# A feed-forward stage with seven block products in place of eight, and its down projection as a second pass

## The chip, the cores and the metric

The kernel runs on one core of a Trainium2 chip. The metric is the device time of one execution in microseconds (us). One run in the profiler comes with a trace of every instruction on the core's engines: TensorE (PE, matmuls; its weight loads PEld), VectorE (DVE), ScalarE (ACT), GpSimd (POOL) and SyncE (SP, which here only issues DMAs).

## The reference, cut to what matters

The whole is a two-block transformer on 1024 rows (S) of 1024 columns (D) in float32. The change concerns the feed-forward part of the first block, with F = 2816 hidden columns:

```
h = h + xo.reshape(b, s, XA_HEADS * XA_HEAD_DIM) @ xa_w_o[l]

fn = rms_norm(h, norm_ffn[l])
g = fn @ ffn_w_gate[l]
g_pad = jnp.pad(g, ((0, 0), (CONV_W - 1, 0), (0, 0)))
cw = ffn_conv_w[l]
g_conv = ffn_conv_b[l] + sum(cw[i] * g_pad[:, i:i + s] for i in range(CONV_W))
h = h + (jax.nn.silu(g_conv) * (fn @ ffn_w_up[l])) @ ffn_w_down[l]
```

The convolution has three taps along the rows. Cross-attention stands ahead of this part, the second block's even layer behind it.

## The kernel before, in words

Every float32 matmul is made of three passes (`mm3`, lines 258 to 265): each operand is split into a high half, cast by ScalarE, and a low half, the difference, made by VectorE or GpSimd. The passes are high x high, high x low, low x high, all with 128 rows of weights and 512 moving columns, summed in a PSUM bank. `load_w` does this for weights: a DMA on SP (line 192), the cast on ACT (line 197), the subtraction (line 202) with 66% of the columns on DVE and the rest on POOL.

`norm_T` (line 224) scales the rows of h by their norm, transposes them on PE (line 250) and splits them (`split`, ACT line 211, DVE line 212) into X: 8 k blocks of 128 x 1024, high and low. `ffn` (line 312) then goes through F in 11 groups of 256 columns. For each group it loads gate and up weights (two loads of 512 KB each) and two blocks of down weights. For each of the two f tiles of 128 hidden columns PE makes gate into a two-bank PSUM tile `pb` (48 matmuls), ACT adds the bias and the third tap (line 329), DVE the other two taps from PSUM (line 331), ACT the silu (line 333); PE makes up (48 matmuls), DVE multiplies (line 336), ACT and POOL split y into halves (lines 339, 340). The down projection of the group before stands between the gate products: `out_proj` makes 16 banks of 6 matmuls, and DVE adds each to h in place (line 290), which stays in SBUF throughout. The list of instructions is put into an order for each engine by a scheduler that goes by program order and priorities (`later` shifts a part of it); a DMA queue and an engine take what they have in that order, and an instruction that waits holds up all behind it.

Behind the stage, the next one stores h in `hs` (line 1815), norms and transposes it, and reads its own weights `a_w_in` and small convolution weights by SP.

## Time and profile before

| | |
|---|---|
| median of 3 runs | 3114.76 us (3112.94 to 3118.19) |
| the profiled run | 3115.11 us |
| its span in the trace | 3113.4 us, mean granted TensorE clock 0.984 |
| busy: TensorE, VectorE, ScalarE, GpSimd | 2959.9, 1958.0, 1128.7, 839.4 us |
| DMA | 228.44 MB, 73 GB/s over the span |
| feed-forward stage, from its first transpose to the next stage's | 758.62 to 1499.00 us |

The profile's page sums the run; the views of the trace behind it show a stretch of time (windows), single instructions on an engine in order of time with the idle time before each and what ended it (timeline), and groups of instructions by line and shape (lines). A matmul's printed duration is the time from its start to its modelled end; matmuls overlap, so their spacing is read from counts in a window or from starts.

### The profile page before, as it was taken

Reading aid. Unit: us, or ns where it says so; the run is one execution under the profiler, and the core shown is the slowest. Engines: PE = TensorE matmul, PEld = TensorE weight load, DVE = VectorE, ACT = ScalarE, POOL = GpSimd, SP = SyncE. Lnnn points to the kernel's source line nnn. Section 1 sums busy time; section 2 is a strip of 40 time slices with the busy share of each in tenths; the row PEclk is TensorE's granted clock in tenths of the full one; section 3 lists DMA queues with packets and bytes.
Section 4 is the critical chain, followed back from the end, with each engine's and each line's share of the span. In section 5 each row is a group of like instructions: output and inputs, shape, how many; then the busy total and the mean of one; then the engine's idle time right before and its main releaser. Section 6 shows DMA issues by size and latency. Waiting matters only on the chain.

```text
span 3113.4 us, 38565 instructions
## 1 busy us (share of the span) xinstructions
PE 2959.9 (95%) x14726; PEld 2413.3 (78%) x14734; DVE 1958.0 (63%) x3129; ACT 1128.7 (36%) x2090; POOL 839.4 (27%) x754
## 2 busy tenths in 40 slices
...
DMA packets 167565, 228.44 MB, mean 73 GB/s; under 512 B 15293, under 2 KB 105941, under 8 KB 167381
## 3 DMA queue, kind: packets, MB, share of 16 engines
...
q8 instruction: 116, 1.90, 0.3%
...
## 4 chain that ended last, share of the span: by engine, by line
PE 68%; DVE 14%; issue 5%; POOL 4%; DMA 3%; ACT 3%; SPq 0%; POOLq 0%; DVEq 0%; ACTq 0%
PE pa_t L263 11%; PE pa_t L264 11%; PE pa_t L265 11%; PE pb_t L265 8%; PE pb_t L264 8%; PE pb_t L263 8%; DVE acc_t L1144 3%; PE pa_t L774 2%; PE pb_t L869 1%; DVE wl_t L202 1%; PE pa_t L888 1%; PE pb_t L1583 1%; DVE h_t L290 1%; DMA wr_t<-in_c_w_in 1%; PE pb_t L1584 1%
## 5 line engine op out<-in xcount | busy, mean ns | idle before, releaser
L202 POOL TENSOR_TENSOR wl_t<-wr_t,wh_t 128x349 fp32r<-128x349 f32 (+2 forms) x221 | 296.9, 1346 | 1311.5 <-ACT wh_t L197 1252.6
L263 PE MATMUL pb_t<-x_t,wh_t 128*128 128x512 f32 x1312 | 518.8, 396 | 3.7 <-DVE bc_t L1184 1.1
L265 PE MATMUL pb_t<-x_t,wl_t 128*128 128x512 f32 x1312 | 516.2, 394 | 0.8 <-DVE wl_t L202 0.8
L264 PE MATMUL pb_t<-x_t,wh_t 128*128 128x512 f32 x1280 | 505.4, 395 | 0.0
L197 ACT CAST wh_t<-wr_t 128x1024 fp32r<-128x1024 f32 (+2 forms) x221 | 217.5, 993 | 546.8 <-PE pb_t L264 240.1
L202 DVE TENSOR_TENSOR wl_t<-wr_t,wh_t 128x675 fp32r<-128x675 f32 (+1 forms) x195 | 208.6, 1074 | 303.2 <-ACT wh_t L197 302.8
L263 PE MATMUL pa_t<-wh_t,x_t 128*128 128x512 f32 (+3 forms) x1024 | 374.5, 366 | 2.6 <-DVE xl_t L212 0.8
L264 PE MATMUL pa_t<-wl_t,x_t 128*128 128x512 f32 (+3 forms) x1024 | 371.3, 363 | 0.5 <-DVE wl_t L202 0.5
L1144 DVE SCALAR_TENSOR_TENSOR acc_t<-u_t,c,acc_t 128x1024 f32<-128x1024 f32 x240 | 339.7, 1417 | 2.9
L290 DVE TENSOR_TENSOR h_t<-h_t,pa_t 128x512 f32<-128x512 f32 x336 | 226.4, 684 | 147.7 <-PE pa_t L265 145.9
L263 PEld LDWEIGHTS pb_t<-x_t,wh_t 128*128 128x128 f32 x1312 | 247.6, 189 | 58.8 <-ACT x_t L211 1.9
L265 PEld LDWEIGHTS pb_t<-x_t,wl_t 128*128 128x128 f32 x1312 | 247.5, 189 | 55.6 <-DVE wl_t L202 2.1
L264 PEld LDWEIGHTS pb_t<-x_t,wh_t 128*128 128x128 f32 x1280 | 241.4, 189 | 52.7 <-DVE x_t L212 0.9
L265 PE MATMUL pa_t<-wh_t,x_t 128*128 128x512 f32 (+3 forms) x640 | 221.5, 346 | 0.0
L263 PEld LDWEIGHTS pa_t<-wh_t,x_t 128*128 128x128 f32 x1024 | 192.3, 188 | 33.9 <-ACT wh_t L197 2.2
L264 PEld LDWEIGHTS pa_t<-wl_t,x_t 128*128 128x128 f32 x1024 | 192.5, 188 | 31.3 <-DVE wl_t L202 2.2
L265 PE MATMUL pa_t<-wh_t,xl_t 128*128 128x512 f32 x512 | 200.9, 393 | 3.0 <-POOL xl_t L1681 2.1
L263 PE MATMUL pa_t<-wh_t,g_t 128*128 128x512 f32 x384 | 150.1, 391 | 2.6 <-DVE h_t L292 1.3
L264 PE MATMUL pa_t<-wl_t,g_t 128*128 128x512 f32 x384 | 149.4, 389 | 0.0
L265 PE MATMUL pa_t<-wh_t,g_t 128*128 128x512 f32 x352 | 136.8, 389 | 1.1 <-POOL g_t L340 1.1
L209 DVE TENSOR_TENSOR pt_t<-pa_t,pt_t 128x512 fp32r<-128x512 f32 (+2 forms) x240 | 119.7, 506 | 24.0 <-ACT pt_t L208 22.1
L208 ACT CAST pt_t<-pa_t 128x512 fp32r<-128x512 f32 (+2 forms) x240 | 104.8, 443 | 81.0 <-PE pa_t L774 44.9
...
## 6 DMA issues: line engine op xcount, KB each, us to landing
wr_t<-in_a_w_in SPq DMA_DIRECT2D x46, 512.0 KB
wr_t<-in_c_w_in SPq DMA_DIRECT2D x26, 512.0 KB
wr_t<-in_ffn_w_gate SPq DMA_DIRECT2D x22, 512.0 KB
wr_t<-in_ffn_w_up SPq DMA_DIRECT2D x22, 512.0 KB
wr_t<-in_ffn_w_down SPq DMA_DIRECT2D x22, 512.0 KB
h_t<-in_x SPq DMA_DIRECT2D x16, 512.0 KB
wr_t<-in_a_w_out SPq DMA_DIRECT2D x16, 512.0 KB
...
```

The costliest lines, as they stand in the source:

```text
L197: nc.scalar.copy(hi, raw)
L202: e.tensor_tensor(*[x[:, c] for x in f], op=ALU.subtract)
L208: nc.scalar.copy(hi, src)
L209: nc.vector.tensor_tensor(lo, src, hi.bitcast(F32), op=ALU.subtract)
L263: mm(out, lh, rh, start=st, stop=False)
L264: mm(out, lh, rl, start=False, stop=False)
L265: mm(out, ll, rh, start=False, stop=en)
L290: self.nc.vector.tensor_tensor(h[t][:, c], h[t][:, c], ps, op=ALU.add)
L774: self.nc.tensor.transpose(pt[:, i * 256 + q * P:i * 256 + (q + 1) * P], w[t0 + q][:, (b0 + i) * P:(b0 + i + 1) * P], self.ident)
L869: mm(sp[:, c0:c0 + wd], qT[:96, hd, t * P:(t + 1) * P], kT[:96, hd, c0:c0 + wd], start=True, stop=c0 + wd < n)
L888: mm(po[:, q:256], vhl[hd][:, kb], x[:, i * 256 + q:i * 256 + 256], start=kb == 0 and j == 0, stop=kb == t0 + 1 and j == 1)
L1144: nc.vector.scalar_tensor_tensor(acc, u[:, k:k + S], cw31(k, c), acc, op0=ALU.mult, op1=ALU.add)
```

## The change

Gate and up of a group are computed as one 256 x 1024 (weight columns x rows) result each, split 2 x 2: two halves of 128 columns, two halves of 512 rows, and the inner dimension in two halves of 512. In place of eight block products there are seven, by Strassen's scheme in Winograd's form, with weights A and activations B: A11 B11, A12 B21, S2 T2, S3 T3, S1 T1, A22 T4, S4 B22. The weight sums are S1 = A21 + A22, S2 = S1 - A11, S3 = A11 - A21, S4 = A12 - S2; the activation sums T1 = B12 - B11, T2 = B22 - T1, T3 = B22 - B12, T4 = T2 - B21. The results are sums of products, taken out of PSUM by VectorE.

`ffn_w` makes the seven weight operands of a unit (gate or up of a group) with their halves. `ffn_x` makes the activation operands; the scaled rows are made in place, so h is first stored to DRAM (`hf`). `ffn_up` runs the 22 units; y of each pair of f tiles is stored to DRAM (`yf`). `ffn_down` is a second pass: y is read back, split, and multiplied by the down weights in groups of four f tiles (12 matmuls in a bank; the last group has two tiles and 6), with h read back from `hf`. PSUM banks are single ones from `pa`. Lines behind the stage move by 167 or 176.

```diff
@@ -309,40 +309,207 @@
-    def ffn(self, h, st):
...
+    def ffn_w(self, dram, c0):
+        nc = self.nc
+        r = []
+        for i in range(2):
+            r.append(self.slot("wr", [P, 4, 256]))
+            nc.sync.dma_start(out=r[i], in_=dram[i * 512:i * 512 + 512, c0:c0 + 256].rearrange("(k p) n -> p k n", p=P))
+        a11, a21, a12, a22 = (x[:, :, o:o + P] for x in r for o in (0, P))
+        out = {}
+        v, g = nc.vector, nc.gpsimd
+        def halves(name, src, eng):
+            hi, lo = out[name] = self.slot("wh", [P, 4, P], F32R), self.slot("wl", [P, 4, P], F32R)
+            nc.scalar.copy(hi, src)
+            eng.tensor_tensor(lo, src, hi.bitcast(F32), op=ALU.subtract)
+        halves("A11", a11, v)
+        halves("A22", a22, g)
+        s1, s2, s3, s4 = a22, a11, a21, a12
+        g.tensor_tensor(s1, a21, a22, op=ALU.add)
+        g.tensor_tensor(s3, a11, a21, op=ALU.subtract)
+        g.tensor_tensor(s2, s1, a11, op=ALU.subtract)
+        halves("S2", s2, v)
+        halves("A12", a12, v)
+        g.tensor_tensor(s4, a12, s2, op=ALU.subtract)
+        halves("S3", s3, v)
+        halves("S1", s1, v)
+        halves("S4", s4, g)
+        return out
+    def ffn_x(self, h, st, hf, between):
+        nc = self.nc
+        X = {n: [[x[:, i] for i in range(2)] for x in (self.slot(tag, [P, 2, 512], F32R) for _ in range(4))]
+             for n, tag in (("B11", "x"), ("B21", "x"), ("B22", "xz"))}
+        th = {n: [self.slot("xh", [P, 512], F32R) for _ in range(4)] for n in ("T2", "T3", "T1", "T4")}
+        X.update({n: [] for n in th})
+        rows = [[self.slot("xt", [P, 512]) for _ in range(2)] for _ in range(4)]
+        gs = list(st)
+        for t in [g0 + j for g0 in gs for j in range(4)]:
+            nc.gpsimd.dma_start(out=hf[t * P:(t + 1) * P, :], in_=h[t])
+        v = nc.vector
+        def turn(g0, k):
+            ps = self.psum()
+            for j in range(4):
+                nc.tensor.transpose(ps[:, j * P:(j + 1) * P], h[g0 + j][:, k * P:(k + 1) * P], self.ident)
+            return ps
+        def halves(n, k, src, eng):
+            hi, lo = th[n][k], self.slot("xt", [P, 512], F32R)
+            X[n].append((hi, lo))
+            nc.scalar.copy(hi, src)
+            eng.tensor_tensor(lo, src, hi.bitcast(F32), op=ALU.subtract)
+        for i, g0 in enumerate(gs):
+            with self.later(0 if i else -AHEAD):
+                for j in range(4):
+                    t = h[g0 + j]
+                    if j == 3:
+                        nc.scalar.activation(t, t, AF.Copy, scale=st[g0][:, j:j + 1])
+                    else:
+                        v.tensor_scalar(t, t, st[g0][:, j:j + 1], None, op0=ALU.mult)
+                for k in range(4):
+                    c1, c2 = self.col("norm_ffn", k), self.col("norm_ffn", k + 4)
+                    p1, p2 = turn(g0, k), turn(g0, k + 4)
+                    if i == 0:
+                        for n, p, c, r in (("B11", p1, c1, rows[k][0]), ("B21", p2, c2, rows[k][1])):
+                            self.split(*X[n][k], p, c)
+                            nc.scalar.activation(r, p, AF.Copy, scale=c)
+                        continue
+                    ta, tb = (self.slot("wr", [P, 2, 512]) for _ in range(2))
+                    t1, t2, t3, t4 = ta[:, 0], ta[:, 1], tb[:, 0], tb[:, 1]
+                    b11, b21 = rows[k]
+                    v.scalar_tensor_tensor(t1, p1, c1, b11, op0=ALU.mult, op1=ALU.subtract)
+                    v.scalar_tensor_tensor(t2, p2, c2, t1, op0=ALU.mult, op1=ALU.subtract)
+                    self.split(*X["B22"][k], p2, c2)
+                    nc.gpsimd.tensor_tensor(t3, t2, b11, op=ALU.subtract)
+                    nc.gpsimd.tensor_tensor(t4, t2, b21, op=ALU.subtract)
+                    halves("T2", k, t2, v)
+                    halves("T3", k, t3, v)
+                    halves("T1", k, t1, v)
+                    halves("T4", k, t4, nc.gpsimd)
+            if i == 0:
+                between(X)
+        return X
+    def ffn_up(self, h, st, hf, yf, cw, more):
+        v = nc.vector
+        ha, hb = (slice(g0 * P, g0 * P + 512) for g0 in st)
+        units = [(x, g) for g in range(DFF // 256) for x in ("ffn_w_gate", "ffn_w_up")]
+        ws, p1 = {}, {}
+        def load(i):
+            if i < len(units):
+                ws[i] = self.ffn_w(a[units[i][0]][0], units[i][1] * 256)
+            elif i == len(units):
+                self.wd = self.down_w(0)
+        def prod(w, x):
+            ps = self.psum()
+            for k in range(4):
+                self.mm3(ps, [(w[0][:, k], w[1][:, k])], [x[k]], k == 0, k == 3)
+            return ps
+        def first(i, X):
+            p1[i] = self.slot("p1", [P, 512])
+            nc.scalar.copy(p1[i], prod(ws[i]["A11"], X["B11"]))
+        load(0)
+        load(1)
+        def between(X):
+            for i in range(2):
+                first(i, X)
+            for i in range(2):
+                p2[i] = prod(ws[i]["A12"], X["B21"])
+        p2 = {}
+        X = self.ffn_x(h, st, hf, between)
+        more()
+        gt = {}
+        for i, (kind, g) in enumerate(units):
+            gate = kind == "ffn_w_gate"
+            if gate:
+                G = [self.slot("g", [P, S]) for _ in range(2)]
+            else:
+                O = gt.pop(g)
+            def part(j, hs, u, ps, op=ALU.add):
+                x = G[j][:, hs] if gate else self.tmp(512)
+                v.tensor_tensor(x, u, ps, op=op)
+                if not gate:
+                    nc.gpsimd.tensor_tensor(O[j][:, hs], O[j][:, hs], x, op=ALU.mult)
+            def total(u, ps):
+                x = self.tmp(512)
+                v.tensor_tensor(x, u, ps, op=ALU.add)
+                return x
+            if i > 1:
+                first(i, X)
+            w = ws.pop(i)
+            u2 = total(p1[i], prod(w["S2"], X["T2"]))
+            part(0, ha, p1[i], p2[i] if i < 2 else prod(w["A12"], X["B21"]))
+            if i:
+                load(i + 1)
+            u3 = total(u2, prod(w["S3"], X["T3"]))
+            p5 = prod(w["S1"], X["T1"])
+            part(1, hb, u3, p5)
+            u4 = total(u2, p5)
+            part(1, ha, u3, prod(w["A22"], X["T4"]), ALU.subtract)
+            part(0, hb, u4, prod(w["S4"], X["B22"]))
+            if gate:
+                gt[g] = []
+                for j in (0, 1):
+                    f = 2 * g + j
+                    o = self.slot("o", [P, S])
+                    nc.scalar.activation(o, G[j], AF.Identity, scale=cw(2, f), bias=self.col("ffn_conv_b", f))
+                    for tap, sh in ((1, 1), (0, 2)):
+                        v.scalar_tensor_tensor(o[:, sh:], G[j][:, :S - sh], cw(tap, f), o[:, sh:], op0=ALU.mult, op1=ALU.add)
+                    nc.scalar.activation(o, o, AF.Silu)
+                    gt[g].append(o)
+            else:
+                for j in (1, 0):
+                    nc.sync.dma_start(out=yf[2 * g + j], in_=O[j])
+    def down_w(self, f0):
+        out = {}
+        for hf in range(2):
+            for f in range(f0, min(f0 + 4, DFF // P)):
+                out[f, hf] = self.load_w(self.a["ffn_w_down"][0], f * P, 1, hf * 512, 512), 0
+        return out
+    def ffn_down(self, hs, yf):
+        nc = self.nc
+        h, st = [], {}
+        for f0 in range(0, DFF // P, 4):
+            fs = range(f0, min(f0 + 4, DFF // P))
+            w = self.wd if f0 == 0 else self.down_w(f0)
+            for f in fs:
+                y = self.slot("yr", [P, S])
+                nc.sync.dma_start(out=y, in_=yf[f])
+                hl = [self.slot("yb" if f0 % 8 else "ya", [P, S], F32R) for _ in range(2)]
+                nc.scalar.copy(hl[0], y)
+                (nc.gpsimd if f % 2 else nc.vector).tensor_tensor(hl[1], y, hl[0].bitcast(F32), op=ALU.subtract)
+                ys.append(hl)
+            if f0 == 0:
+                h = self.load_h(hs, nc.scalar)
+            last = f0 + 4 >= DFF // P
+            for x, ts in ([(range(2), [t]) for t in range(NT)] if last else [([hf], range(NT)) for hf in range(2)]):
+                for hf in x:
+                    self.out_proj(h, ys, [w[f, hf] for f in fs], ts=ts, hfs=[hf], stats=st if last and hf else None)
+        return h, st
...
@@ -1802,8 +1969,17 @@
         if h_in is None or "B" in stages:
             mctx.close()
         if "C" in stages:
-            with K.pool("xf", x=16), K.pool("w1", wr=2, wh=6, wl=6), K.pool("ffn", g=10, tmp=2):
-                st = K.ffn(h, st)
+            hf, yf = dt("hf", [S, D]), dt("yf", [DFF // P, P, S])
+            with K.pool("wf", wr=3, wh=10, wl=10, p1=2):
+                cw = K.convw("ffn_conv_w", 3, DFF, tag="wr")
+                with K.pool("xf", x=8, xh=16, xt=16, xz=4), ExitStack() as fs:
+                    def more():
+                        hctx.close()
+                        fs.enter_context(K.open(K.pool("fg", o=2, tmp=4, g=2)))
+                    K.ffn_up(h, st, hf, yf, cw, more)
+                hctx = K.open(K.pool("h1b", "right", h=8))
+                with K.pool("fd", yr=2, ya=8, yb=8):
+                    h, st = K.ffn_down(hf, yf)
         if "D" in stages:
             with K.pool("w1", **W), K.pool("xd", usum=1, rsg=4, g=3, acc=2):
                 usum, rs = K.slot("usum", [P, S]), []
```

The removed `ffn` is printed above with the kernel before. Line numbers in what follows are those of each kernel.

The order of the instructions, first on PE where the stage begins. Line 250 is the transposes before, line 359 after; 263 to 265 are the three passes. Before:

```order
L250 MATMUL pa_t<-c_72,g_t 128x128
L263 MATMUL pa_t<-wh_t,x_t 128x512
L250 MATMUL pa_t<-c_72,g_t 128x128
L264 MATMUL pa_t<-wl_t,x_t 128x512
L250 MATMUL pa_t<-c_72,g_t 128x128
L265 MATMUL pa_t<-wh_t,x_t 128x512
L250 MATMUL pa_t<-c_72,g_t 128x128 x45
L263 MATMUL pb_t<-x_t,wh_t 128x512 x2
```

After, where the first half's transposes and then those of the second half stand:

```order
L263 MATMUL pa_t<-x_t,wh_t 128x512
L264 MATMUL pa_t<-x_t,wh_t 128x512
L265 MATMUL pa_t<-x_t,wl_t 128x512
L359 MATMUL pa_t<-c_72,h_t 128x128 x32
L263 MATMUL pa_t<-xh_t,wh_t 128x512
L264 MATMUL pa_t<-xt_t,wh_t 128x512
L265 MATMUL pa_t<-xh_t,wl_t 128x512
```

The second half's transposes have moved behind the early products of units 0 and 1 (a further 32 of line 359 stand ahead of those), where before all but a few stood together.

DVE in the middle of the stage. Before, line 331 is the taps from PSUM `pb_t`, 336 the multiplication, 290 the sum into h, 202 the low halves of weights:

```order
L202 TENSOR_TENSOR wl_t<-wr_t,wh_t 128x675 x2
L331 SCALAR_TENSOR_TENSOR g_t<-pb_t,c_6941,g_t 128x1023
L331 SCALAR_TENSOR_TENSOR g_t<-pb_t,c_6941,g_t 128x1022
L202 TENSOR_TENSOR wl_t<-wr_t,wh_t 128x675
L336 TENSOR_TENSOR g_t<-g_t,pb_t 128x1024
L202 TENSOR_TENSOR wl_t<-wr_t,wh_t 128x675
L331 SCALAR_TENSOR_TENSOR g_t<-pb_t,c_6941,g_t 128x1023
L290 TENSOR_TENSOR h_t<-h_t,pa_t 128x512 x2
L331 SCALAR_TENSOR_TENSOR g_t<-pb_t,c_6941,g_t 128x1022
```

After, 448 and 454 are the sums with a product's bank `pa_t`, 477 the taps from SBUF, 327 the low halves; the first row still belongs to a gate unit, those behind the taps to the up unit:

```order
L454 TENSOR_TENSOR tmp_t<-tmp_t,pa_t 128x512
L327 TENSOR_TENSOR wl_t<-wr_t,wh_t 128x512
L448 TENSOR_TENSOR g_t<-tmp_t,pa_t 128x512 x2
L327 TENSOR_TENSOR wl_t<-wr_t,wh_t 128x512
L477 SCALAR_TENSOR_TENSOR o_t<-g_t,c_6793,o_t 128x1023 x2
L477 SCALAR_TENSOR_TENSOR o_t<-g_t,c_6793,o_t 128x1022 x2
L454 TENSOR_TENSOR tmp_t<-p_t,pa_t 128x512
L327 TENSOR_TENSOR wl_t<-wr_t,wh_t 128x512 x2
L448 TENSOR_TENSOR tmp_t<-p_t,pa_t 128x512
L327 TENSOR_TENSOR wl_t<-wr_t,wh_t 128x512
L454 TENSOR_TENSOR tmp_t<-tmp_t,pa_t 128x512
```

The taps of both f tiles now stand in a row ahead of the up unit's first sum, and nothing sums into h.

SP around the turn from up to down, after only (482 stores y, 501 loads it back, 192 loads down weights); there is nothing like it before:

```order
L482 DMA yf<-o_t 128x1024 x2
L192 DMA wr_t<-in_ffn_w_down 128x512 x11
L482 DMA yf<-o_t 128x1024
L501 DMA yr_t<-yf 128x1024
L482 DMA yf<-o_t 128x1024
L501 DMA yr_t<-yf 128x1024
L192 DMA wr_t<-in_ffn_w_down 128x512
```

SP where the next stage begins, before:

```order
L192 DMA wr_t<-in_ffn_w_down 128x1024 x2
L192 DMA wr_t<-in_a_w_in 128x8x128 x2
L192 DMA wr_t<-in_a_w_in 128x3x256
L192 DMA wr_t<-in_a_w_in 128x3x16
L192 DMA wr_t<-in_a_w_in 128x3x256
L192 DMA wr_t<-in_a_w_in 128x3x16
L192 DMA wr_t<-in_a_w_in 128x2x256
L192 DMA wr_t<-in_a_w_in 128x2x16
L192 DMA wr_t<-in_a_w_in 128x8x128
L162 DMA g_t<-in_a_conv_w 64x128
```

and after:

```order
L501 DMA yr_t<-yf 128x1024
L192 DMA wr_t<-in_ffn_w_down 128x512 x7
L162 DMA g_t<-in_a_conv_w 64x128
L162 DMA g_t<-in_a_dw_w 128x128
L162 DMA g_t<-in_a_dw_w 120x128
L192 DMA wr_t<-in_a_w_in 128x8x128 x2
```

The three small loads of line 162 now stand ahead of all of the next stage's weight loads instead of behind nine of them. In the kernel after, the first of them waits for the last down matmul of the stage.

## Rows read from the trace of the kernel before

**Rows 1.** Page: busy us (share) and instructions by engine; then the chain

```profile
PE 2959.9 (95%) x14726; PEld 2413.3 (78%) x14734; DVE 1958.0 (63%) x3129; ACT 1128.7 (36%) x2090; POOL 839.4 (27%) x754
...
PE 68%; DVE 14%; issue 5%; POOL 4%; DMA 3%; ACT 3%; SPq 0%; POOLq 0%; DVEq 0%; ACTq 0%
```

**Rows 2.** A window: stretch, length, busy PE, PEld, DVE, ACT, POOL, clock, DMA

```profile
980.00:1180.00 200.00, 200.00 (x884) 165.62 (x883) 77.39 (x87) 38.29 (x36) 39.24 (x24) 1.00 0.16 48
```

**Rows 3.** Timeline of PE, the stage begins: start, us, what, idle before

```profile
758.62 0.27 PE L250 MATMUL pa_t<-c,g_t 128*128 128x128 f32 x1
...
759.66 1.60 PE L250 MATMUL pa_t<-c,g_t 128*128 128x128 f32 x13
...
770.82 3.78 PE L250 MATMUL pa_t<-c,g_t 128*128 128x128 f32 x16 [5.39 <-DVE g_t L245]
774.41 1.22 PE L263 MATMUL pb_t<-x_t,wh_t 128*128 128x512 f32 x2
```

**Rows 4.** Windows as in rows 2: after that idle stretch, and elsewhere

```profile
770.00:772.00 2.00, 1.18 (x6) 1.04 (x6) 2.00 (x5) 1.90 (x2) 0.77 (x1) 0.50 0.84 259
...
774.00:776.00 2.00, 2.00 (x7) 1.14 (x6) 2.00 (x4) 2.00 (x4) 1.46 (x1) 0.50 0.63 166
...
1630.00:1640.00 10.00, 8.07 (x32) 5.54 (x32) 9.94 (x9) 6.68 (x21) 5.31 (x4) 0.83 0.02 5
```

**Rows 5.** Timeline of PE where the stage ends

```profile
1480.70 0.73 PE L265 MATMUL pa_t<-wh_t,g_t 128*128 128x512 f32 x2 [1.10 <-POOL g_t L340]
...
1498.76 0.40 PE L265 MATMUL pa_t<-wh_t,g_t 128*128 128x512 f32 x1
1499.00 0.90 PE L250 MATMUL pa_t<-c,h_t 128*128 128x128 f32 x4
...
1501.87 0.50 PE L263 MATMUL pb_t<-x_t,wh_t 128*128 128x512 f32 x1
```

**Rows 6.** Groups by line and shape: count, busy us, mean ns, idle before

```profile
L290 DVE TENSOR_TENSOR h_t<-h_t,pa_t 128x512 f32<-128x512 f32 x336 | 226.4, 684 | 147.7 <-PE pa_t L265 145.9 <-issue 1.2
L202 DVE TENSOR_TENSOR wl_t<-wr_t,wh_t 128x675 fp32r<-128x675 f32 x190 | 205.6, 1087 | 259.4 <-ACT wh_t L197 259.2
...
L340 POOL TENSOR_TENSOR g_t<-g_t 128x1024 fp32r<-128x1024 f32 x22 | 53.0, 2411 | 148.8 <-ACT g_t L339 148.8
...
L202 POOL TENSOR_TENSOR wl_t<-wr_t,wh_t 128x512 fp32r<-128x512 f32 x26 | 36.6, 1410 | 82.6 <-ACT wh_t L197 61.4 <-PE pa_t L774 8.8 <-PE pa_t L264 4.1
...
L331 DVE SCALAR_TENSOR_TENSOR g_t<-pb_t,c,g_t 128x1023 f32<-128x1023 f32 x22 | 28.2, 1283 | 116.0 <-ACT g_t L329 116.0
...
L197 ACT CAST wh_t<-wr_t 128x512 fp32r<-128x512 f32 x28 | 17.3, 626 | 10.4 <-PE pa_t L264 5.5 <-PE pa_t L265 2.2 <-DMA wr_t<-in_c_w_in 2.2
```

**Rows 7.** Timeline of POOL and DVE: subtractions apart (first, last) and beside each other

```profile
764.53 0.92 POOL L202 TENSOR_TENSOR wl_t<-wr_t,wh_t 128x349 fp32r<-128x349 f32 x1 [54.58 <-ACT wh_t L197]
...
1443.65 3.07 DVE L202 TENSOR_TENSOR wl_t<-wr_t,wh_t 128x675 fp32r<-128x675 f32 x2
...
1443.54 2.46 POOL L202 TENSOR_TENSOR wl_t<-wr_t,wh_t 128x349 fp32r<-128x349 f32 x2 [28.26 <-ACT wh_t L197]
...
1483.63 0.85 DVE L202 TENSOR_TENSOR wl_t<-wr_t,wh_t 128x675 fp32r<-128x675 f32 x1
```

**Rows 8.** DMA issues: queue, count, KB each, median us from issue to landing

```profile
hs<-h_t POOLq DMA_DIRECT2D x8, 512.0 KB, 4.5
```

**Rows 9.** Timeline of SP and ACT: a weight load and its cast; stage end

```profile
766.31 2.67 SPq L192 DMA_DIRECT2D wr_t<-in_ffn_w_up  x2
...
770.11 1.05 ACT L197 CAST wh_t<-wr_t 128x1024 fp32r<-128x1024 f32 x1 [2.39 <-DMA wr_t<-in_ffn_w_up]
...
1484.55 9.90 SPq L192 DMA_DIRECT2D wr_t<-in_a_w_in  x7
1494.50 0.59 SPq L162 DMA_DIRECT2D g_t<-in_a_conv_w  x1
1495.13 1.07 SPq L162 DMA_DIRECT2D g_t<-in_a_dw_w  x2
```

35 lines of the change are left out of this document (2 added, 33 removed).

## The prediction

> **What bounds the kernel now.** I read the page first. TensorE is busy for 2959.9 of 3113.4 us, VectorE for 63%, GpSimd for 27%, and 68% of the chain of work that ended last lies on TensorE [rows 1]. So a matmul that goes away should shorten the run, as long as the stage it leaves has no other limit. Next, the windows inside the stage: between 980 and 1180 us TensorE is busy for all 200 us at a granted clock of 1.00 with 884 matmuls [rows 2]. That gives 200/884 = 0.2262 us per 128x512 matmul at the full clock (2.4 GHz). The 395 ns that the page prints for one is how long it is in the pipeline, not the spacing. Then the two borders of the stage in the timeline of TensorE. Its first transpose starts at 758.62, there is one idle stretch of 5.39 us, the first feed-forward matmul is at 774.41 [rows 3]; the last one starts at 1498.76, the next stage's transposes at 1499.00 and its first matmul at 1501.87 [rows 5]. The stage lasts 1499.0 - 758.6 = 740.4 us. Its matmuls are 11 groups x (192 gate and up + 96 down) = 3168, and 3168 x 0.2262 = 716.7 us. The other 23.7 us are 64 transposes (13 took 1.60 us at the full clock just before the idle stretch, so 64 take 7.8 us), 1.1 us of waiting at the end [rows 5], and so 14.8 us of idle time and low clock at the start.
>
> **Term 1, matmuls removed.** A unit is gate or up of one group. Before it has 2 f tiles x 2 halves x 8 k x 3 = 96 matmuls of 128x512, after it 7 products x 4 k x 3 = 84. Over 22 units 264 go: 264 x 0.2262 = **-59.7 us**. The down projection keeps its 1056 matmuls. All 264 stood in a stretch in which TensorE never waited [rows 2], so this gain is whole unless another engine now sets the pace (term 3).
>
> **Term 2, start of the stage.** The Strassen operands of both sequence halves have to be made before unit 0 can end. GpSimd has 24 operations of 128x512: six for each of two units' weights, three for each of four k for the activations. The nearest row is a subtraction at this shape on GpSimd, 1.41 us [rows 6]. From its first operation, at 764.53 before [rows 7], it is through at 764.5 + 24 x 1.41 = 798.4 us if it never waits. In that time TensorE has 64 transposes (7.8 us), the four early products, three more and three quarters of the next (7.75 x 12 x 0.2262 = 21.0 us), so 39.8 - 28.8 = 11.0 us idle or slow, against 14.8 now: -3.8 us. But GpSimd does wait. The second half's transposes stand behind the four early products, and those behind the 8 casts and 8 copies of ScalarE that make the first half; the first operand can be ready by about 773.6, the four products are through at about 783, and the first sums reach GpSimd at about 786. With 12 operations and one cast to wait for, that is 786 + 17 + 1 = 804 us, or +1.8 us. With GpSimd at 1.80 us (two pieces of 349 columns beside VectorE took 2.46 us, 1.23 each; times 512/349) [rows 7] it is 4.7 us later: +6.5. I take the middle, **+4 us**; range -4 to +10, the upper end with the 24 operations at 1.80 us and those waits on top.
>
> **Term 3, the steady part.** A gate and an up unit take 2 x 84 x 0.2262 = 38.0 us of TensorE. Beside it GpSimd has 16 operations: 12 for weights, 4 multiplications; at 1.41 us 22.6 us, at 1.80 us 28.8 us. VectorE has 10 weight subtractions (128x512; the 128x675 one took 0.85 us alone, 1.09 on average [rows 6, 7], so 0.65 to 0.83 each), 14 sums with a PSUM bank at 0.684 us and 4 convolution taps at 1.28 us (the row's read PSUM, the new ones SBUF) [rows 6]: 6.5 + 9.6 + 5.1 = 21.2, up to 23 us. ScalarE has 14 casts at 0.63 us [rows 6] and six other operations, under 16 us. None is full, so throughput is no limit. Latency nearly is. In the up unit VectorE must do the four taps before the sum that frees a PSUM bank, the taps wait for the gate's convolution on ScalarE, and that stands behind the cast of S2 of the next weights, which waits for four GpSimd operations in a row (low half of A22, s1, s3, s2). By the mean rows that sum is done 11.4 us into the unit and TensorE wants its bank at 13.6: 2.2 us of slack. With 1.80 us on GpSimd and the slower subtractions, 4 x 0.39 + 4 x 0.18 = 2.3 us of it go. So a stall of 0 to 1 us per pair, 11 pairs: **+3 us**, 0 to +11.
>
> **Term 4, turn to the down pass.** Before, y stays in SBUF. Now it comes back from DRAM through two slots, and the first load stands on SyncE behind the store of the last pair's tile, which waits for the last up unit. Load and landing took 770.11 - 766.31 = 3.8 us for the same 512 KB [rows 9]. After the last product: f0 lands at 3.8, cast 1.05 and VectorE's low half of 1024 columns (0.85 x 1024/675 = 1.3), 6.2 us; f1, behind the second store, lands at 7.0, is cast at 8.0, and GpSimd's low half takes 2.41 us [rows 6], 10.4; f2 has to wait for f0's slot, lands at 10.0 and is ready at 12.4; f3 waits for f1's slot, lands at 14.2, ready at 17.7. TensorE takes four banks of each tile as it comes, 48 matmuls or 10.9 us, and is through at about 19: **+8.3 us** idle. Lower bound 6 (GpSimd's low halves in 1.3 us, as VectorE's), upper bound 16 (landing in 4.5 us, as the stores of hs [rows 8], and queued weights and h in between). Later groups last 4 x 3 x 16 x 0.2262 = 43.4 us and load ahead; the sums into h fall from 176 operations of 0.684 us to 96. Both are hidden.
>
> **Term 5, border to the next stage.** Before, SyncE issued the last seven of nine weight loads of the next stage from 1484.55, ahead of the small convolution loads at 1494.50 [rows 9]. After, the convolution loads stand first and wait for the last feed-forward matmul, with the weight loads behind them. So from the end: issues 0.59 + 1.07 us [rows 9], landing 3.8, cast 1.05, low half 0.85 = 7.4 us to the first matmul, against 1501.87 - 1499.00 = 2.9 now [rows 5]: **+4.5 us**, 3 to 7. The stores of h to DRAM (eight, on GpSimd) and their reload lie beside other work.
>
> **Term 6, a wait removed.** The 1.10 us for the low half of the last y [rows 5]: **-1.1 us**.
>
> **Term 7, clock.** After the idle stretch of 5.39 us the granted clock read 0.50 (1.2 GHz) from 770 to 776 [rows 4], and a gap of 1.9 us elsewhere leaves 0.83 over ten microseconds [rows 4], which is 10 x 0.17 = 1.7 us of matmul time each. The change makes three new gaps (second half of the start, turn, border). Price 1.7 us each: **+5 us**, 0 where TensorE waits for data anyway, 8 with the longer dip.
>
> **Sum.** -59.7 + 4 + 3 + 8.3 + 4.5 - 1.1 + 5 = -36.0. The profiled run took 3115.1 us (span 3113.4), 0.3 above the median of 3114.8. So 3079.1, and against the median **3078.8 us**. All low ends: -59.7 - 4 + 0 + 6 + 3 - 1.1 + 0 = -55.8, 3059; all high ends: -59.7 + 10 + 11 + 16 + 7 - 1.1 + 8 = -8.8, 3106.
>
> **Rivals.** (a) The borders are hidden better than I walk them: terms 2 to 5 and 7 at or near their low ends; 3059 to 3066. For it: half of these prices rest on loads that land in 3.8 us with nothing beside them. Against: f0's load is tied to the last store by queue order, so some wait is certain.
> (b) VectorE and GpSimd hold each other up in each pair. Two pieces each, 0.85 and 0.92 us alone, took from 1443.54 to 1446.72 = 3.18 us together, nearly their serial sum of 3.54 [rows 7]. After, 14 of VectorE's 28 operations per pair and all 16 of GpSimd's read two SBUF tensors. If half of the nine in the critical chain of term 3 wait out one of the other engine (4 x 0.69 + 5 x 1.3 = 9.3 us, half 4.6), the stall is 4.6 - 2.2 = 2.4 us per pair, 27 us in all: 3079 - 3 + 27 = 3103. For it: the rows just named. Against: 21 to 23 us and 22.6 us of work in 38 leave room.
> The Trainium skill ("SBUF — State Buffer", "Who interferes with whom") states it harder: a VectorE operation with two SBUF inputs and a GpSimd operation that reads SBUF exclude each other for the whole instruction. The pair of rows above comes within a tenth of that. Taken whole, the rule would give the time of rival (c); the rows alone bear out the half of it that (b) has.
> (c) Slower: the same chain, every operation blocked once. Then 9.3 - 2.2 = 7.1 us of stall per pair, 78 us in all, and 3079 - 3 + 78 = 3154 us. It decides from (36 + 3)/11 = 3.5 us of stall per pair, so from 5.7 of those 9.3 us. Against: for this every one of nine operations must meet one of the other engine at its start, while each engine is idle for four tenths of the pair.
> (d) The gain is eaten up to nothing, (b) near its deciding point with the turn at its high end; 3109 to 3121.
>
> **How the numbers follow.** My forecast, the sum with its terms inside their bounds, 3066 to 3090: 0.55. (a) 0.16, (b) 3090 to 3106: 0.19, (d) 0.03, (c) 0.07. The range 3060 to 3104 leaves out (c), (d) and the edges of (a) and (b). A measurement of this kernel can tell 0.2% (6.2 us) from no change: faster 0.90, same 0.03, slower 0.07.
>
> **What would show it.** Windows between the new stage's second and tenth pair: TensorE busy throughout at 1.00 with a period of 38.0 us per pair confirms terms 1 and 3; waits of its matmuls on VectorE's sums, at one place per pair, confirm (b). The timeline at the turn: idle of about 8 us that waits for the halves of y confirms term 4; at the end about 7 us between the last feed-forward matmul and the next stage's first, waiting for its weight load, confirms term 5. Mean durations of GpSimd's 128x512 operations above 1.8 us, or VectorE's subtractions above 0.85 us, would make me wrong towards (b) and (c).

## The result, and the profile after

| | before | after |
|---|---|---|
| median | 3116.35 us (3112.94 to 3118.19, 4 runs) | 3095.55 us (3092.55 to 3098.77, 4 runs) |
| ratio, 95% interval | | 0.9935 [0.9917, 0.9952] |
| the profiled run, its span | 3115.11, 3113.4 us | 3093.24, 3091.2 us |
| feed-forward stage, first transpose to the next stage's | 740.38 us | 717.64 us |
| all around it | 2373.0 us | 2373.6 us |

The change makes the kernel faster by 20.8 us. The forecast was 36.0 us. The time lies in the range, and 16.8 us above the forecast (1.6 of them because the kernel before, too, read higher this time: 3116.35 against 3114.76).

The instructions ahead of and behind the stage, nearly the same in all these kernels, took between 2373.0 and 2386.6 us in the profiled runs; so what an edit does inside the stage is read from the stage's length in the trace, and the medians of most single edits (3091.96 to 3098.77 us) hardly differ from after's. Two kernels with the same stage repeat it within 1 to 2 us (717.64 and 716.69; 702.19 and 703.98), and the part behind the first down matmul alone lasts 243.2 to 245.1 us in seven kernels that have it alike; a difference of 2 us in one trace is therefore not clear of noise.

The page of after, as [rows 1]: TensorE has 14470 instructions in place of 14726 and is busy for 52.7 us less, while every other engine has more to do. (It is 256 fewer and not 264 because the trace of before lacks eight matmuls, whose weight loads it has: x14734.)

```profile
PE 2907.2 (94%) x14470; PEld 2364.7 (76%) x14470; DVE 2062.9 (67%) x3296; ACT 1196.4 (39%) x2264; POOL 1014.5 (33%) x917
```

Windows of after, with the columns of [rows 2]: the start of the stage in five pieces, then the steady pairs, the turn to the down pass, and the down pass.

```profile
768.00:780.00 12.00, 3.89 (x12) 2.75 (x12) 8.49 (x10) 6.97 (x13) 6.47 (x5) 0.50 0.15 44
780.00:784.00 4.00, 4.00 (x12) 3.15 (x11) 0.75 (x1) 2.77 (x5) 3.56 (x3) 0.57 0.00 0
790.00:810.00 20.00, 9.83 (x46) 7.36 (x46) 17.26 (x21) 9.47 (x16) 12.41 (x10) 0.68 0.00 1
810.00:838.00 28.00, 22.36 (x92) 16.87 (x90) 20.39 (x22) 10.96 (x16) 12.96 (x10) 0.99 0.24 75
838.00:842.00 4.00, 3.93 (x10) 3.19 (x11) 3.09 (x6) 2.11 (x3) 2.86 (x2) 0.57 0.39 115
850.00:1210.00 360.00, 360.00 (x1590) 298.20 (x1589) 210.32 (x267) 128.63 (x191) 200.06 (x151) 1.00 0.25 83
1230.00:1250.00 20.00, 16.32 (x55) 11.45 (x56) 4.93 (x6) 5.24 (x5) 4.75 (x2) 0.83 0.93 343
1250.00:1470.00 220.00, 220.00 (x972) 182.25 (x971) 100.28 (x135) 41.49 (x59) 52.09 (x47) 1.00 0.26 89
```

The reader is to see three things. The steady part and the down pass are full: TensorE is busy for all 360 and all 220 us at a clock of 1.00. The turn's window has 3.7 us idle and a clock of 0.83; the idle time begins 3.8 us ahead of that window. And the start is ragged for 74 us: at 790 to 810 TensorE works for half the time, VectorE for 17.26 of 20 us.

The stage as a sum, with 0.2267 us per matmul (139 products of 12 took 378.24 us, start to start): 2904 matmuls are 658.3 us, the 64 transposes 7.8 [rows 3], together 666.1. The other 51.5 us are 40.0 at the start and 11.5 at the turn (these parts are rounded by 0.1 to 0.2). Before, 3168 matmuls were 718.2 and the transposes 7.8, with 13.3 lost at the start and 1.1 at the end [rows 5]. So the change is -59.9 for matmuls, +26.7 at the start, +11.5 at the turn, -1.1 at the end: -22.8 us, where the stage lengths give -22.7.

The timeline of TensorE in after at the start (start, us, what, idle before and its releaser), to be held against [rows 3]:

```profile
759.43 1.54 PE L359 MATMUL pa_t<-c,h_t 128*128 128x128 f32 x12
...
774.91 1.11 PE L359 MATMUL pa_t<-c,h_t 128*128 128x128 f32 x4 [5.98 <-ACT xt_t L382]
778.15 0.80 PE L263 MATMUL pa_t<-x_t,wh_t 128*128 128x512 f32 x1 [2.13 <-ACT xt_t L382]
...
800.65 1.97 PE L359 MATMUL pa_t<-c,h_t 128*128 128x128 f32 x8 [4.55 <-DVE wr_t L387]
806.78 1.11 PE L359 MATMUL pa_t<-c,h_t 128*128 128x128 f32 x4 [4.16 <-DVE wr_t L387]
...
838.07 0.80 PE L263 MATMUL pa_t<-xh_t,wh_t 128*128 128x512 f32 x1 [4.76 <-DVE tmp_t L454]
```

The first feed-forward matmul starts 18.7 us after the first transpose, against 15.8 before, although only half of the transposes stand ahead of it now. Taken apart: 14.8 us are lost up to that matmul, 14.7 from there to the first product of the second half's operands (S2 T2 at 807.63), and 10.4 from there to 847.94, after which TensorE no longer waits until the turn.

**Loss one, ScalarE's order.** The timeline of ScalarE in after:

```profile
767.08 0.68 ACT L382 ACTIVATE xt_t<-pa_t,c 128x512 f32<-128x512 f32 x1
...
772.10 2.18 ACT L326 CAST wh_t<-wr_t 128x512 fp32r<-128x512 f32 x4 [3.75 <-POOL wr_t L334]
774.18 0.68 ACT L382 ACTIVATE xt_t<-pa_t,c 128x512 f32<-128x512 f32 x1
```

The casts of unit 0's weight sums (line 326) stand ahead of the copies that empty the transposes' banks (line 382). They wait 3.75 us for GpSimd's sums; TensorE waits 5.98 us behind them, and the granted clock reads 0.50 and then 0.57 up to 784.

**Loss two, VectorE and GpSimd at the second half.** The timelines of both engines in after over one k of the second half:

```profile
799.20 0.74 DVE L388 SCALAR_TENSOR_TENSOR wr_t<-pa_t,c,wr_t 128x512 f32<-128x512 f32 x1
799.86 0.74 DVE L387 SCALAR_TENSOR_TENSOR wr_t<-pa_t,c,xt_t 128x512 f32<-128x512 f32 x1
800.70 0.75 DVE L212 SCALAR_TENSOR_TENSOR xz_t<-pa_t,c,xz_t 128x512 fp32r<-128x512 f32 x1
801.36 4.04 DVE L366 TENSOR_TENSOR xt_t<-wr_t,xh_t 128x512 fp32r<-128x512 f32 x3
805.33 0.74 DVE L388 SCALAR_TENSOR_TENSOR wr_t<-pa_t,c,wr_t 128x512 f32<-128x512 f32 x1
...
800.09 1.27 POOL L390 TENSOR_TENSOR wr_t<-wr_t,xt_t 128x512 f32<-128x512 f32 x1 [1.36 <-DVE wr_t L388]
...
803.32 1.54 POOL L366 TENSOR_TENSOR xt_t<-wr_t,xh_t 128x512 fp32r<-128x512 f32 x1 [0.73 <-ACT xh_t L365]
```

One k takes 805.33 - 799.20 = 6.13 us, and VectorE is busy throughout: three operations of 0.75 us and three low halves of 1.35 us each. A subtraction of the same kind (128x512, two SBUF inputs) takes 0.68 us when GpSimd stands still (the row at 818.29 below). GpSimd is the one that waits, 1.36 and 0.73 us per k.

**Loss three, the third unit's weights.** The timelines of SyncE, ScalarE, GpSimd and VectorE in after, up to the 4.76 us wait at 838.07:

```profile
811.63 0.37 SPq L319 DMA_DIRECT2D wr_t<-in_ffn_w_gate  x1
...
817.83 0.37 SPq L319 DMA_DIRECT2D wr_t<-in_ffn_w_gate  x1
...
821.57 0.62 ACT L326 CAST wh_t<-wr_t 128x512 fp32r<-128x512 f32 x1 [4.89 <-PE pa_t L264]
827.68 1.67 ACT L326 CAST wh_t<-wr_t 128x512 fp32r<-128x512 f32 x3 [5.49 <-POOL wr_t L334]
830.26 2.38 ACT L475 ACTIVATE o_t<-g_t,c,c 128x1024 f32<-128x1024 f32 x2 [0.91 <-DVE g_t L448]
...
822.27 1.29 POOL L327 TENSOR_TENSOR wl_t<-wr_t,wh_t 128x512 fp32r<-128x512 f32 x1 [5.05 <-ACT wh_t L326]
...
818.29 0.68 DVE L327 TENSOR_TENSOR wl_t<-wr_t,wh_t 128x512 fp32r<-128x512 f32 x1
...
831.54 5.87 DVE L477 SCALAR_TENSOR_TENSOR o_t<-g_t,c,o_t 128x1023 f32<-128x1023 f32 x4
837.34 0.67 DVE L454 TENSOR_TENSOR tmp_t<-p_t,pa_t 128x512 f32<-128x512 f32 x1
```

This is the chain that term 3 of the prediction walks: low half of A22, three sums, the cast of S2, the gate's convolution on ScalarE behind it, four taps on VectorE, and only then the sum that gives TensorE its bank. It stalls once, in the first pair, because the weights of unit 2 come late; in the ten later pairs it stalls nowhere.

The timeline of TensorE in after at the turn, then SyncE's and ScalarE's:

```profile
1232.00 0.79 PE L263 MATMUL pa_t<-wh_t,ya_t 128*128 128x512 f32 x1 [5.82 <-ACT ya_t L503]
...
1241.34 0.50 PE L263 MATMUL pa_t<-wh_t,ya_t 128*128 128x512 f32 x1 [0.62 <-ACT ya_t L503]
...
1246.82 0.74 PE L265 MATMUL pa_t<-wh_t,ya_t 128*128 128x512 f32 x2 [1.02 <-POOL ya_t L504]
...
1226.08 0.33 SPq L482 DMA_DIRECT2D yf<-o_t  x1
1226.46 0.42 SPq L501 DMA_DIRECT2D yr_t<-yf  x1
...
1230.90 1.04 ACT L503 CAST ya_t<-yr_t 128x1024 fp32r<-128x1024 f32 x1 [4.25 <-DMA yr_t<-yf]
```

The first load of y is issued 0.38 us behind the store in front of it and its cast starts 4.44 us later. And the timeline of TensorE at the end of the stage, to be held against [rows 5]:

```profile
1477.07 1.91 PE L250 MATMUL pa_t<-c,h_t 128*128 128x128 f32 x16
...
1485.09 0.51 PE L263 MATMUL pb_t<-x_t,wh_t 128*128 128x512 f32 x1 [1.97 <-ACT wh_t L197]
```

1485.09 - 1477.07 = 8.0 us to the next stage's first matmul, against 2.9.

### The profile page after: what moved, and what is told of

Same layout as the page of the kernel before. It is cut to its first block, busy times and chain, and to the rows that moved or that the text cites. A ratio compares the mean times of both kernels' runs of the same rounds, so it can differ in the third digit from the quotient of the medians.

```text
span 3091.2 us, 39184 instructions
## 1 busy us (share of the span) xinstructions
PE 2907.2 (94%) x14470; PEld 2364.7 (76%) x14470; DVE 2062.9 (67%) x3296; ACT 1196.4 (39%) x2264; POOL 1014.5 (33%) x917
## 4 chain that ended last, share of the span: by engine, by line
PE 66%; DVE 15%; issue 5%; POOL 4%; ACT 3%; DMA 3%; SPq 0%; POOLq 0%; ACTq 0%; DVEq 0%
PE pa_t L263 16%; PE pa_t L264 16%; PE pa_t L265 15%; PE pb_t L265 3%; PE pb_t L264 3%; PE pb_t L263 3%; DVE acc_t L1311 3%; PE pa_t L941 2%; PE pb_t L1036 1%; PE pa_t L1055 1%; DVE wl_t L202 1%; PE pb_t L1750 1%; PE pb_t L1751 1%; ACT wh_t L197 1%; DVE h_t L292 1%
## 5 line engine op out<-in xcount | busy, mean ns | idle before, releaser
L202 POOL TENSOR_TENSOR wl_t<-wr_t,wh_t 128x349 fp32r<-128x349 f32 (+3 forms) x199 | 239.0, 1207 | 976.0 <-ACT wh_t L197 942.2
L202 DVE TENSOR_TENSOR wl_t<-wr_t,wh_t 128x675 fp32r<-128x675 f32 (+2 forms) x173 | 170.9, 991 | 169.1 <-ACT wh_t L197 168.6
L263 PE MATMUL pb_t<-x_t,wh_t 128*128 128x512 f32 x608 | 244.3, 402 | 3.7 <-ACT wh_t L197 2.9
L265 PE MATMUL pb_t<-x_t,wl_t 128*128 128x512 f32 x608 | 242.2, 399 | 1.0 <-DVE wl_t L202 1.0
L264 PE MATMUL pb_t<-x_t,wh_t 128*128 128x512 f32 x576 | 231.0, 401 | 0.0
L263 PE MATMUL pa_t<-x_t,wh_t 128*128 128x512 f32 x400 | 163.9, 410 | 2.8 <-ACT xt_t L382 2.1
L265 PE MATMUL pa_t<-x_t,wl_t 128*128 128x512 f32 x400 | 158.8, 397 | 0.0
L263 PE MATMUL pa_t<-xh_t,wh_t 128*128 128x512 f32 x352 | 138.9, 395 | 5.3 <-DVE tmp_t L454 4.8
L263 PEld LDWEIGHTS pb_t<-x_t,wh_t 128*128 128x128 f32 x608 | 115.5, 190 | 30.8 <-ACT wh_t L197 3.9
L264 PE MATMUL pa_t<-xt_t,wh_t 128*128 128x512 f32 x352 | 138.2, 392 | 0.4 <-DVE xt_t L366 0.4
L265 PE MATMUL pa_t<-xh_t,wl_t 128*128 128x512 f32 x352 | 137.8, 392 | 0.0
```

Source lines behind the costliest of these rows:

```text
L202: e.tensor_tensor(*[x[:, c] for x in f], op=ALU.subtract)
L263: mm(out, lh, rh, start=st, stop=False)
L264: mm(out, lh, rl, start=False, stop=False)
L265: mm(out, ll, rh, start=False, stop=en)
```

## The experiments

All diffs are against the kernel after. Intervals are of the ratio to the kernel before.

### The matmuls alone

```diff
...
-            part(0, hb, u4, prod(w["S4"], X["B22"]))
+            part(0, hb, u4, prod(w["S4"], X["B22"], 2))
```

`prod` with a 2 runs its 12 matmuls twice into the same bank: the 264 matmuls are back, the rest of the change stays.

> The last of the seven products of each unit is summed twice over in the same bank (24 matmuls in place of 12), so that the 264 matmuls that the change took out are back and all else of the new stage stays; that result is then not the reference's. My theory: the steady part is paced by TensorE alone, so all of 264 x 0.2267 = 59.8 us comes back: about 3152 to 3156 us, some 37 us slower than the kernel before, which is what the two ends of the stage cost. Rival (the seven products save less, because VectorE, GpSimd or the chain between them set part of the pace): the new matmuls fill waits, and less than 50 us comes back.

Measured: 3164.49 us, ratio 1.0148 [1.0127, 1.0169], above the 3152 to 3156 expected. The timeline of TensorE in this kernel where the stage begins and ends:

```profile
766.94 1.54 PE L359 MATMUL pa_t<-c,h_t 128*128 128x128 f32 x12
...
1549.48 1.91 PE L250 MATMUL pa_t<-c,h_t 128*128 128x128 f32 x16
```

The stage lasts 782.54 us, 64.9 more than after. From S2 T2 to the first down matmul it is 480.66 us against 424.37, 56.3 more. There the full 264 x 0.2267 = 59.9 us are back but for 3.6, and the first pair's wait (3.07 in place of 4.76) and the turn's first wait (3.49 in place of 5.82) are shorter by 4.0 beside the longer work. So the gain of term 1 is whole. Another 9.0 us stand behind the first down matmul (254.1 against 245.1), where this kernel has no more work: four further waits for the halves of y take 6.3 us together, in place of two that take 1.6, and the granted clock reads 0.81 from 1286 to 1306 and 0.89 over the 44 us behind. Why y comes later here was not tried apart. The stage is 42.2 us longer than before: the 37.1 of the edges in the sum above, less those 4.0 and with these 9.0.

### The start: ScalarE's order

```diff
...
+        if later is not None:
+            g.tensor_tensor(s4, a12, s2, op=ALU.subtract)
+            later.append(lambda: [halves(*x) for x in (("S2", s2, v), ("S3", s3, v), ("S1", s1, v), ("S4", s4, g))])
+            return out
...
-        load(1)
...
+            with self.later(100):
+                rest[0]()
+            load(1)
```

The casts of unit 0's sums move behind the first half's copies, and unit 1's weights behind them.

> One part of the start undone: the casts of unit 0's weight sums (S2, S3, S1, S4) stand behind the first half's casts and copies in ScalarE's order, not between them, and unit 1's weights follow. My theory: the first product waited for ScalarE, which was stuck behind a cast that waits for three GpSimd sums; it starts about 13.5 us after the stage's first transpose, not 18.7, and the stage is 4 to 6 us shorter. Rival (GpSimd's 24 operations pace the start, whatever the order): the later sums only move the wait to the second half, and the stage is within 1.5 us of what it was.

Measured: 3098.77 us, 0.9945 [0.9930, 0.9960]; stage 719.42, +1.8 where -4 to -6 was forecast. The first product starts 12.0 us after the first transpose in place of 18.7, and nothing is won: TensorE then waits 3.27 and 1.17 us for ScalarE's casts of weights (line 326) between the early products, and S2 T2 starts at +49.9 (after: +48.2). The wait on ScalarE was real, and it was not the pace: the weights that it is moved past wait next.

### The start: one low half from VectorE to GpSimd

```diff
-                    halves("T1", k, t1, v)
+                    halves("T1", k, t1, nc.gpsimd)
```

> One subtraction for each k (the low half of T1) goes from VectorE to GpSimd; nothing is left out. My theory: the second half's operands come every 6.1 us because VectorE has six operations for each k (2.25 us plus three low halves at 1.3 us beside GpSimd); with five it is about 5.0 to 5.4 us, GpSimd then being about even, and the stage is 2 to 4 us shorter. Rival (GpSimd paces): the period grows to about 6.1 + 1.3 = 7.4 us and the stage is about 5 us longer.

Measured: 3096.54 us, 0.9935 [0.9912, 0.9958]; stage 714.40, -3.2, and one k takes 5.81 us and not 5.0 to 5.4. That -3.2 lies inside the forecast is luck: 1.9 of it stand behind the first down matmul, where the edit changes nothing, and the 1.3 ahead of it are not clear of noise. The timelines of VectorE and GpSimd in this kernel:

```profile
797.47 3.38 DVE L366 TENSOR_TENSOR xt_t<-wr_t,xh_t 128x512 fp32r<-128x512 f32 x2
800.77 0.74 DVE L388 SCALAR_TENSOR_TENSOR wr_t<-pa_t,c,wr_t 128x512 f32<-128x512 f32 x1
...
806.58 0.74 DVE L388 SCALAR_TENSOR_TENSOR wr_t<-pa_t,c,wr_t 128x512 f32<-128x512 f32 x1
...
797.36 1.28 POOL L391 TENSOR_TENSOR wr_t<-wr_t,xt_t 128x512 f32<-128x512 f32 x1
798.65 3.33 POOL L366 TENSOR_TENSOR xt_t<-wr_t,xh_t 128x512 fp32r<-128x512 f32 x2
```

From 797.36 to 801.98 stand three operations of GpSimd and two of VectorE, all with two SBUF inputs: 4.62 us, where one after the other they would take 3 x 1.28 + 2 x 0.69 = 5.2. About a ninth of the work overlapped. So two engines did here hardly more than one, and moving a half between them relieves little. The Trainium skill ("SBUF — State Buffer", "Who interferes with whom") says that such operations exclude each other; the trace agrees but for that ninth.

### The start: without the sums beside it

```diff
-                    nc.gpsimd.tensor_tensor(t3, t2, b11, op=ALU.subtract)
-                    nc.gpsimd.tensor_tensor(t4, t2, b21, op=ALU.subtract)
-                    halves("T3", k, t3, v)
+                    halves("T3", k, t2, v)
-                    halves("T4", k, t4, nc.gpsimd)
+                    halves("T4", k, t1, nc.gpsimd)
```

The eight sums T3 and T4 on GpSimd are left out; every half is still made.

> The sums T3 and T4 of the start, eight GpSimd operations, are left out; the products take the halves of T2 and T1 in their place, so the result is not the reference's. VectorE's work is the same as in the changed kernel. My theory: VectorE's low halves of the start are slow (1.31 us, 0.69 alone) because GpSimd reads SBUF beside them; without the eight sums they take 0.7 to 0.95 us, the operands of one k come every 4.3 to 5.2 us in place of 6.1, and the stage is 4 to 7 us shorter. Rival (VectorE is slow here on its own account, by the kind of output or the address): 1.3 us and 6.1 us stay.

Measured in a single run: 3087.32 us; stage 706.24, -11.4, more than forecast (1.3 of it behind the first down matmul). One k takes 3.97 us in place of 6.13. The groups by line of VectorE in the second half of the start, of after and then of this kernel (count, busy us, mean ns):

```profile
L366 DVE TENSOR_TENSOR xt_t<-wr_t,xh_t 128x512 fp32r<-128x512 f32 x12 | 15.1, 1310 | 0.0
```

```profile
L366 DVE TENSOR_TENSOR xt_t<-wr_t,xh_t 128x512 fp32r<-128x512 f32 x12 | 8.6, 773 | 0.0
```

VectorE's 12 low halves fall from 1310 to 773 ns by taking away work of another engine: 6.4 us. TensorE's waits on VectorE's sums at the second half fall with them, from 10.0 to 5.8 us, S2 T2 comes 4.1 us earlier, and the first pair's wait goes from 4.76 to 1.92. So the two engines do hold each other up, and 4.1 of the 14.7 us of loss two are shown to be that; most of the waits that are left, 5.8 us, stand beside the six operations per k that VectorE has anyway, and the low clock beside them. Loss three hangs on the same sums ending late: unit 2's two loads go out 43.0 and 48.0 us into the stage, in place of 52.2 and 58.4.

### The start: the early products among the second half's k

```diff
-            if i == 0:
-                between(X)
+                    between(X, k)
```

The four early products, which need nothing of the second half, no longer stand in front of its transposes: in the program one stands behind each of the second half's k pairs, in the `pb` banks; in the trace TensorE runs their matmuls among the transposes of both halves.

> The four early products of units 0 and 1 no longer stand ahead of the second half's transposes: one of them follows each k of the second half, in the other PSUM banks (pb). Nothing is left out. My theory now: the second half's sums and low halves take VectorE and GpSimd about 6.1 us for each of four k, whatever else is done, and in the changed kernel they started only 32 us into the stage, behind the early products. Started at about 20 us, the first S2 T2 product begins 38 to 42 us into the stage in place of 48, and the stage is 7 to 11 us shorter. Rival (the late point is unit 2's weights, whose loads wait for the slots that the sums hold): the early start only lengthens a later wait, and the stage is less than 3 us shorter.

Measured: 3096.37 us, 0.9930 [0.9910, 0.9950]; stage 712.58, -5.1 in place of 7 to 11. S2 T2 starts at +38.8 as forecast, 9.4 us earlier; half of that is lost behind it, where the last operands and unit 2's weights are no earlier by as much: TensorE now waits 4.4 us inside the first products of the second half (0.4 in after), and the first pair's wait is 2.54 us.

### Sums in place

```diff
-                    ta, tb = (self.slot("wr", [P, 2, 512]) for _ in range(2))
+                    ta = self.slot("wr", [P, 2, 512])
+                    b11, b21 = t3, t4 = rows[k]
...
```

T3 and T4 take the place of the raw rows (but for the last k), so that three slots fewer are held that the weight loads want.

> Only the sums T3 and T4 made in place for three of four k, so that the sums hold five weight slots in turn and not eight, and unit 2's weight loads go out earlier (in the changed kernel the first at 52 us into the stage). My theory: the wait of 4.8 us in the first pair comes from unit 2's weights being late through those slots; the loads go out at 40 to 46 us, the wait falls under 2 us, the stage is 3 to 6 us shorter. Rival (it is the chain of GpSimd, ScalarE and VectorE in every pair, seen first where no lead has been built up): the wait stays at 4 us or more.

Measured in a single run: 3102.55 us; stage 717.20, and the first pair's wait is 4.77 us, as in after. The load of unit 2's weights is issued at 811.18, against 811.63. My theory that these slots held it back falls. What does hold it, SyncE's waits between 780 and 840 us show (total, times, longest), in after and then in this kernel, with the row of ScalarE's cast of A22 in this kernel behind them:

```profile
SPq L319 <- DVE xt_t L366: 41.2, 2, 35.4
```

```profile
SPq L319 <- DVE xt_t L366: 40.2, 2, 34.5
...
821.54 0.62 ACT L326 CAST wh_t<-wr_t 128x512 fp32r<-128x512 f32 x1 [5.39 <-DMA wr_t<-in_ffn_w_gate]
```

Both loads of unit 2's gate weights wait for VectorE's low halves of the second half. In after they go out at 811.63 and 817.83, 0.06 us behind the last low half of the third and of the fourth k (811.57, 817.77); here at 811.18 and 817.30. The edit lets fewer sums take slots, but the two loads still come behind the sums of these k. A22 comes with the second load, and its cast waits for the landing: it starts 4.2 us behind the issue here, 3.7 in after. So loss three begins with the last low half of the start.

### The first pair by eight products

```diff
...
+        if plain:
+            for name, x, eng in (("A11", a11, v), ("A21", a21, g), ("A12", a12, v), ("A22", a22, g)):
+                halves(name, x, eng)
+            return out
...
+                part(0, hb, p1[i], prod(w["A11"], X["T1"], None, (w["A12"], X["B22"])))
+                part(1, hb, q1[i], prod(w["A21"], X["T1"], None, (w["A22"], X["B22"])))
...
```

The first two units need no weight sums and only B11, B21, B22 and T1, for 24 more matmuls. The sums in place and the early loads of y (below) are in it too.

> The turn as in the run with early y loads, the sums T3 and T4 in place, and the first pair of units by eight block products, written so that they need only B11, B21, B22 and T1 of the activations and no weight sums (C12 is A11 B11 + A11 T1 + A12 B22): 24 matmuls more (5.4 us), nothing left out. T2, T3 and T4 are then needed only by the third unit, some 40 us later. My theory (the start's loss, 39.9 us against 13.3 before, is the making of seven operands of each kind before the first units can end): the loss falls to 14 to 20 us, the first pair waits for nothing over 2 us, and the stage is 690 to 697 us against 717.6, so about 3065 to 3078 us. Rival (the loss is set by VectorE's and GpSimd's total work at the start, which the eight products don't cut): the third unit waits instead, and the stage is no better than the 702.2 of the three edits together.

Measured: 3084.32 us, 0.9894 [0.9876, 0.9912]; stage 709.02, where 690 to 697 was forecast. A miss: the wait has moved to the third unit. The two largest groups of TensorE's waits in this kernel, from the stage's start to the turn (total, times, longest):

```profile
PE pa_t L265 <- DVE wl_t L327: 4.0, 1, 4.0
PE pa_t L263 <- DVE tmp_t L466: 3.6, 2, 2.7
```

The longest of each stand at 831.44 and 856.96, where unit 2's first low half and the first sums come; the weights of that unit are loaded at 799.54 and about 822. The median is low beside the stage's length; the intervals of this kernel and of the three edits below overlap.

### The turn: stores on another queue

```diff
-                    nc.sync.dma_start(out=yf[2 * g + j], in_=O[j])
+                    nc.gpsimd.dma_start(out=yf[2 * g + j], in_=O[j])
...
-                with K.pool("fd", yr=2, ya=8, yb=8):
+                with K.pool("fd", yr=4, ya=8, yb=8):
```

> The stores of y go out on GpSimd's queue, so that the first loads of y don't stand behind the last stores on SyncE, and y has four slots in place of two. My theory: the 11.5 us lost at the turn (5.8 us idle, two short waits, and about 5 us of matmuls at half the clock) are queue order and slots; the loads go out while the last products run, and 8 to 11 us come back. Rival (the turn is bound by transfers, y, h and down weights together at over 340 GB/s, or by splitting y): under 4 us.

Measured: 3096.47 us, 0.9937 [0.9919, 0.9954]; stage 714.52, -3.1, the rival's side. One wait of 4.88 us is left. The loads of y are no longer behind a store on SyncE, but at 1227.61 behind twelve loads of down weights that SyncE issues from 1187.11 on, and the DMA engines are full. The window of this kernel at the turn (clock, DMA share, GB/s at the end):

```profile
1230.00:1250.00 20.00, 16.68 (x59) 12.81 (x60) 6.37 (x7) 6.21 (x7) 6.44 (x5) 0.83 1.02 390
```

### The turn: y loaded before it

```diff
...
-                nc.sync.dma_start(out=y, in_=yf[f])
+                with self.later(0 if f0 else -150):
+                    (nc.sync if f0 else nc.sync).dma_start(out=y, in_=yf[f])
...
-                h = self.load_h(hs, nc.scalar)
+                h = self.load_h(hs, nc.gpsimd)
...
+                        hs2.append(K.open(K.pool("yp", "right", yr=2)))
...
```

The two slots of y lie in memory that is free before the turn, its first loads come long before, and h is read by GpSimd's queue. The stores are on GpSimd's queue as above.

> Stores of y on GpSimd's queue as in the run with four slots, but the two slots for y lie in memory that is free during the products, so that the first two loads of y go out long before the last product, and the reload of h goes to GpSimd's queue behind the low halves. My theory, since the four-slot run only gained 3 us at full DMA load (287 to 416 GB/s): at the turn all of y, h and down weights are moved at once, and y is late because of that. With two y tiles there already and h later, the wait at the turn falls from 5.8 us to under 1.5 us, and the stage is 7 to 10 us shorter than in the changed kernel. Rival (splitting y on ScalarE, VectorE and GpSimd, 2.3 to 3.4 us a tile, is what the turn waits for): at least 4 us of the 11.5 stay lost.

Measured: 3091.96 us, 0.9916 [0.9899, 0.9934]; stage 712.36, -5.3, where 7 to 10 was forecast; the first wait falls under 1.5 us as forecast. The timeline of TensorE in this kernel at the turn:

```profile
1228.60 0.50 PE L263 MATMUL pa_t<-wh_t,ya_t 128*128 128x512 f32 x1 [1.47 <-ACT ya_t L504]
...
1231.30 0.50 PE L265 MATMUL pa_t<-wh_t,ya_t 128*128 128x512 f32 x1 [1.02 <-DVE ya_t L505]
...
1237.61 0.50 PE L263 MATMUL pa_t<-wh_t,ya_t 128*128 128x512 f32 x1 [1.04 <-ACT ya_t L504]
```

With the data there, splitting it into halves sets the pace: five waits of 4.5 us together (two more of 0.58 and 0.40 us beside those shown) take the place of 7.5, and the low clock behind the long gap is gone.

### The border

```diff
-        cw4 = self.convw("a_conv_w_2", 4, 2048, 0.5)
-        cw31 = self.convw("a_dw_w_2", 31, 1024, 0.5)
+        with self.later(60):
+            cw4 = self.convw("a_conv_w_2", 4, 2048, 0.5)
+            cw31 = self.convw("a_dw_w_2", 31, 1024, 0.5)
```

Two weight loads of the next stage stand ahead of its convolution weights again.

> Only the border to the next stage: its two first weight loads stand ahead of the small convolution loads on SyncE again. By the prediction's term 5 the late weights cost 4.5 us and more. In the two traces the next stage's first matmul was 5.1 us later after the last feed-forward matmul than before, its long convolution on VectorE began 4.7 us later and ended 2.7 us later. My theory: with two loads first, the first matmul comes 2 to 4 us earlier (under 6 us after the last feed-forward matmul, 8.0 in the changed kernel), and the end of that convolution on VectorE, 652.4 us after the stage's last matmul, comes 0 to 2 us earlier. Rival: the convolution's end doesn't move, and the border costs nothing.

Measured in a single run: 3095.18 us; stage 716.69. The first matmul starts 5.1 us after the stage's end in place of 8.0. What becomes of these 2.9 us is read at the long convolution of the next stage, 240 taps on VectorE (line 1144 before, 1311 after). Its first tap starts 34.9 us after the stage's end in before, 39.6 in after, 36.2 here; its last 649.7, 652.4 and 649.5. The other ten kernels with the border of after have the first tap at 38.8 to 41.6 and the last at 650.3 to 656.7. So at the first tap the border's cost, and this edit's gain of 3.4 us, are clear of the scatter. At the last tap 2.7 us are left in these three traces, less than the 6.4 by which kernels with one border differ there; how much of the cost reaches the end is not shown.

### Together

The interleaved products, the sums in place and the early loads of y in one kernel:

> Three edits together: early products behind each k, y's turn as in the run before, and the sums T3 and T4 made in place for three of four k, so that unit 2's weight loads get their slots earlier; nothing is left out. If start and turn are separate losses, their gains add: 14 to 20 us less than the changed kernel's stage, and with the slots another 3 to 6 (the wait of 4.8 us in the first pair with its slow clock), so a stage of about 695 us in place of 717.6, and about 3072 to 3078 us. If the first pair's wait is the chain of GpSimd, ScalarE and VectorE and not the slots, it stays at 3 us or more.

Measured: 3089.18 us, 0.9910 [0.9891, 0.9929]; stage 702.19, -15.5: a miss, with a stage of about 695 and 3072 to 3078 us forecast. Alone the three gave 5.1, 0.4 and 5.3 us, 4.7 less than together. I put that down to the sums in place, which may be worth something only where the early products are out of the way: unit 2's second load goes out 53.2 us into the stage here, against 55.1 with the interleaved products alone. That is 1.9 us of the 4.7, and the two other edits together without this one were not run. With the border added:

> The edits that acted, together: early products interleaved, sums in place, y loads ahead of the turn, and two weight loads of the next stage ahead of the convolution loads. Theory (the edits lie in different stretches and add): stage 700 to 704 us as with the first three, next stage's first matmul 5 us after the stage's end instead of 7.9, last long-convolution tap 2.9 us earlier relative to the stage's end, and 2.9 us off the median of the three edits' run: 3086 us (3082 to 3090). Rival (the first taps of the next stage wait for convolution weights that now land later, or the two weight loads take slots the stage's last group wants): border 5 us but last tap not earlier than +651 us after the stage's end, median 3089 or more.

Measured: 3079.60 us (3077.91 to 3090.53, 5 runs), 0.9875 [0.9852, 0.9899]; stage 703.98. The first matmul starts 5.1 us after the stage's end, the last long tap at +649.0 against +650.8 without the border's edit. The first taps are not held up by their weights: the first stands at 35.8, and the rival's +651 for the last is not reached. This is the lowest median of all, 37.4 us below before and 16.0 below after, and below the 3082 to 3090 forecast. It is also 9.6 below the kernel without the border's edit, and the traces give that edit 2.9 us at most; the rest of the 9.6 has no cause in them.

## Why the prediction was right or wrong

**Bound and term 1: right.** TensorE bounded the stage and still does; 264 matmuls are worth 59.9 us (forecast 59.7), and the experiment that puts them back shows it.

**Term 2, the start, is the step that failed:** it took GpSimd for the pace and ended with the last operand. Forecast: +4, and 1.7 of clock. Measured: 40.0 - 13.3 = +26.7 us. The 21 us between come from four places:

- 7 us: the first sum reaches GpSimd at 793.96, by the walk at 786 (the stage began 0.8 us later). I had the four early products ready to go at 773.6; ScalarE's casts wait for GpSimd in front of the copies, and the first product starts at 778.15, at half clock. Undone alone it won nothing; with the products out of the second half's way, 9.4 us at S2 T2 and 5.1 in the stage.
- 5 us: from that sum to the last operand it takes 23.2 us (793.96 to 817.2), not the 18 of 12 GpSimd operations and a cast. I took GpSimd for the pace, where VectorE has six operations per k and GpSimd waits for it. The rows for it were named, under rival (b): two pieces beside each other took nearly their serial sum [rows 7]. I used them for the steady part, where both engines have room, and not at the start, where neither has.
- 6.4 us: the first pair's wait of 4.76 and 1.6 of half clock behind it. The walk ended with the last operand and did not ask when the third unit's weights would come; their second load waits for VectorE's last low half (817.77).
- the remaining 2 to 3 us: more low clock than one dip of 1.7 (0.57 at 780 to 784, 0.68 over 790 to 810).

**Term 3, the steady part: +3 forecast, 0 measured.** 360 of 360 us busy, a pair in 38.1 us. The low halves were slower than I allowed on VectorE (907 ns on average over the stage, my mark was 850) and faster than my upper price on GpSimd (1291 ns). The mark was a poor one: with VectorE busy for 58% and GpSimd for 56% of that window, a slower operation does not end last. Rival (b) had the mechanism right and the place wrong; (c) and (d) did not happen, and (a) neither.

**Term 4, the turn: right in its mechanism and near in size.** 8.3 and 1.7 of clock forecast; 7.5 of waits and 4.0 of low clock measured, 11.5 together. The load landed a little later (its cast starts 4.4 us after the issue, 3.8 taken), with the DMA engines at 0.93.

**Term 5, the border: right at its place, not settled at the end.** Forecast +4.5, measured +5.1 (8.0 - 2.9) at the first matmul and 4.8 at the long convolution's first tap. At its last tap 2.7 are left in these traces, inside the scatter. TensorE is not full behind the border (148.4 of 160 us from 1540 on, VectorE 146.3), so part of a late start may be made up; which engine lets it was not tried apart.

**Terms 6 and 7.** The last wait of 1.1 us is gone. The clock's dips are where they were expected, after the gaps at the start and the turn; their prices are in the terms above.

In sum: -59.9 + 26.7 + 0 + 11.5 - 1.1 = -22.8 in the stage; what the border costs behind it can't be told from the rest, which differs by 0.6 us here and by up to 13.6 between other runs. That the range held is luck in part. Its upper reach came from rival (b), and was needed by the start and not by the pairs; and the 21 us that the start was off were partly made up by 3 us of stalls that did not come and by a border whose 4.5 us and clock don't show in the total.
